# Hybrid S5, RG-LRU and GLA block: another order at the first norm, the decay logarithms, the GLA heads and the turn of the feed-forward part

## The chip, the cores and the metric

One core of one Trainium2 chip runs the kernel. The metric is the device time of one execution in microseconds (us), lower is better. Five engines work side by side and wait for each other by semaphores: TensorE (PE, the matmuls), VectorE (DVE), ScalarE (ACT), GpSimd (POOL) and SyncE (SP, which here only issues DMAs). Each takes its instructions in one order fixed beforehand, so an instruction that waits holds up all that stand behind it on its engine.

## What is computed

One layer over 1024 latent tokens and 256 context tokens of width 1024, in float32:

```python
u  = modulate(rms_norm(h, ln1_g), mod[0], mod[1])        # mod = split(silu(c) @ ada_w + ada_b)
zl = split(u @ w_in);  zc = split(uc @ w_in)             # 5408 columns
s5_l  = s5_branch(zc[0], zl[0], ...)                     # 16 groups x 64 complex states, both directions
lru_l = rglru_branch(zc[1], zc[2], zl[1], zl[2], ...)
gla_l = gla_branch(q, k, v, g, z, ...)                   # 4 heads, chunks of 64, both directions
#   log_alpha(z) = log_sigmoid(z @ w2 + b2) / 16
#   per chunk: cum = cumsum(log_alpha); k_out = k * exp(cum_last - cum);  s = decay * s + k_out^T v
m = sigmoid(g0) * (s5_l @ w_s5) + sigmoid(g1) * (lru_l @ w_lru) + sigmoid(g2) * (gla_l @ w_gla)
h = h + mod[2] * (m @ w_out)
u = modulate(rms_norm(h, ln2_g), mod[3], mod[4])
gate, val = split(dwconv(u @ w_up))                      # 2 x 2816 channels
h = h + mod[5] * ((silu(gate) * val) @ w_down)
return rms_norm(h, final_g)
```

## The kernel before

Every float32 operand of a matmul is held as two parts, a rounded high part (`uh`, `wh`) and the remainder (`ul`, `wl`), and a product is three matmuls (high by high, high by low, low by high). The high part of a weight block is a copy with rounding on ACT (L214), the low part a subtraction on POOL or DVE (L215). Tokens lie in two halves of 512 columns, the width in eight tiles of 128 rows.

The program goes through these stages. Times are those of the profiled execution.

- **Start (0 to 41 us).** `START` is a list of steps that fixes the order on all engines by hand. `x` loads a tile, `sq` squares it on ACT, `sa` adds the squares (L389; on DVE, for three steps of the second half on POOL, list `ONPOOL`). `rs`, `re`, `rp`, `rb`, `rc` make the inverse root and spread it over the rows. `a` loads a block of the modulation weights, `ar` multiplies one row of them (eight blocks, L310), `at`, `ac`, `am` turn it into shift and scale. `un` scales a tile (L314), `u` rounds it (L317), `ul` takes the remainder (L320), `m1` and `m2` are the first products (L428, L429).
- **Projections with three mixers.** The projections come from a generator, `proj_stream`, a list of steps each with a cost in us. Whoever builds a mixer calls `F(name)` with a number from the table `FILL`, and `fill` runs so many us of that stream at this place; this lays projection matmuls among the mixer's matmuls on PE. A weight block is taken from a queue of three (`take`).
- **z, v and the decay logarithms (194 to 336 us).** `z_steps` loads the weight block `wz`, splits it (L687, L688), multiplies context (L691, L692) and latent tokens (L699 to L701), and leaves z in SBUF. `v_steps` multiplies v for a list of blocks of 128 tokens: for each half of v it takes two weight blocks at once and fills two PSUM tiles `p` at a time (L726 to L728), then copies them out (L733) and writes them with a DMA on ACT's queue (L734). `decay_logs` runs 12 sets: one matmul `w2` by z (L653), absolute value, relu and exponential on ACT (L658, L660, L661), a polynomial as pairs of a square on ACT (L665) and a multiply-add on DVE (L662, L666), a subtraction on POOL (L667) and a write (L668). `background` strings the sets together, the 512-wide ones first; `advance` runs one step of it after each `BG` us of the stream.
- **S5 (from 335 us).** Transposes (L1166), products and outputs (L1187, L1215, L1245) with long chains on DVE, ACT and back. Logs and S5 share DVE.
- **GLA heads (519 to 900 us).** For each head `decays` runs two scans of 64x1280 (L1287, L1288), copies, exponentials (L1295 to L1297) and `ko` = exp (L1299, L1300). `states` runs 18 dependent steps on DVE (L1362) and copies the states (L1365, L1366). `nxt.decays()` of the next head is called after `head.scores(0)`. Projections go on beside it: L528 to L532 the products, L795 their evacuation by ACT through a tanh.
- **Output projection and second norm (900 to 930 us).** L284 to L286 multiply, L1722 adds to `h`. At `m == 1` of the second half the loop makes the normed first half, and POOL subtracts tiles 0 to 3 from tiles 4 to 7 (L1752).
- **The turn (930 to 986 us)** goes from this into the feed-forward part. Each pair of 128-row channel tiles is built by seven products with sums of weights and of activations (a fast scheme; `Pair`, products `p1` to `p7` with operands `B11`, `B21`, `B22`, `T1` to `T4`). The order on DVE, ACT and POOL is written by hand there (`norm_order`). `c1`, `z6`, `z57` copy and add PSUM results into `gv`; in `z57` the first instruction is a copy on ACT (L1666).
- **Main loop and end (986 to 1600 us)**: pairs 2 to 21, the down product, the last norm.

## Time and profile before

| | us |
|---|---|
| median of 3 runs | 1599.78 |
| lowest, highest | 1599.44, 1605.92 |
| the profiled execution | 1601.49 |
| its span, first to last instruction | 1599.7 |
| PE busy | 1521.8 (95%) |
| DVE busy | 1092.8 (68%) |
| ACT busy | 770.1 (48%) |
| POOL busy | 461.3 (29%) |
| mean granted clock of TensorE | 0.983 |

The span is what the trace shows; 1.8 us of the execution lie around it. PE is busy nearly all the time, so the time is that of PE's matmuls and of the places where PE waits or runs at the lower clock. The table of waits names for each wait the instruction that waited and the one that released it. A granted clock of 1.00 is 2.4 GHz, 0.50 is 1.2 GHz.

### The profile page before, as it was taken

The page shows a single profiled execution, that of the slowest core. Times are in us where ns is not written, and L with a number is a line of the kernel's source. Part 1 is how long each engine was busy: PE and PEld are TensorE (multiplying, and loading weights), DVE is VectorE, ACT ScalarE, POOL GpSimd, SP SyncE. Part 2 cuts the span into 40 slices and gives each one's busy share as a digit, 9 for nine tenths or more (in the row PEclk, how much of TensorE's full clock was granted, in tenths as well). Part 3 has the DMA queues.
Part 4 walks back from the last instruction along what each step waited for, and adds up shares of the span by engine and source line. Part 5 has one row for each costly group of instructions (what it writes and reads, how often), then busy time and mean ns, then how long its engine had stood idle before and what let it go on. Part 6 is the DMA issues. An engine that isn't in the chain of part 4 may idle for free. (4 is left out here: it accounts for less than half of the span.)

```text
span 1599.7 us, 21566 instructions
## 1 busy us (share of the span) xinstructions
PE 1521.8 (95%) x8144; PEld 1254.7 (78%) x8144; DVE 1092.8 (68%) x1620; ACT 770.1 (48%) x1221; POOL 461.3 (29%) x291
## 2 busy tenths in 40 slices
PE   5999999799998999999999988999999999999997
PEld 4888867677886788788888767788888888878887
DVE  4533469879876624533461689888888888899962
ACT  4423766665543643443233455444444444444661
POOL 3313333431122323222236534333333333000032
PEclk9999999899999999999999999999999999999999
DMA  9763633221224244231474321222222222974203
GB/s 346 242 224 93 208 109 110 93 90 58 64 61 144 70 139 130 77 86 60 144 246 159 130 88 40 92 80 79 80 91 81 80 80 100 370 248 157 93 27 106
DMA packets 93785, 198.91 MB, mean 124 GB/s; under 512 B 13489, under 2 KB 34865, under 8 KB 93553
## 3 DMA queue, kind: packets, MB, share of 16 engines
q1 hardware_dynamic: 81968, 181.62, 33.9%
q10 hardware_dynamic: 11712, 15.91, 2.9%
q8 instruction: 64, 1.05, 0.3%
q14 instruction: 41, 0.33, 0.1%
HBM read 158.98 MB, written 38.52 MB: 123 GB/s over the span
## 5 line engine op out<-in xcount | busy, mean ns | idle before, releaser
L215 POOL TENSOR_TENSOR wl<-wr,wh 128x1024 fp32r<-128x1024 f32 (+2 forms) x87 | 183.4, 2109 | 455.7 <-ACT wh L214 428.5
L214 ACT CAST wh<-wr 128x1024 fp32r<-128x1024 f32 (+2 forms) x87 | 77.3, 891 | 139.6 <-issue 41.9
L215 POOL TENSOR_TENSOR wp<-tmp,wp 128x512 fp32r<-128x512 f32 x44 | 74.1, 1701 | 220.4 <-ACT wp L214 203.4
L528 PE MATMUL ma<-uh,wh 128*128 128x512 f32 x272 | 118.0, 434 | 4.5 <-ACT pt L795 4.5
L528 PE MATMUL mb<-uh,wh 128*128 128x512 f32 x272 | 107.2, 394 | 0.0
L530 PE MATMUL ma<-ul,wh 128*128 128x512 f32 x272 | 107.0, 393 | 0.0
L530 PE MATMUL mb<-ul,wh 128*128 128x512 f32 x272 | 106.9, 393 | 0.0
L532 PE MATMUL mb<-uh,wl 128*128 128x512 f32 x272 | 106.7, 392 | 0.0
L532 PE MATMUL ma<-uh,wl 128*128 128x512 f32 x272 | 106.4, 391 | 0.0
L214 ACT CAST wp<-tmp 128x512 fp32r<-128x512 f32 x78 | 46.5, 619 | 93.0 <-DVE tmp L1629 92.9
L1693 DVE SCALAR_TENSOR_TENSOR ca<-gv,vec,ca 128x1023 f32<-128x1023 f32 (+2 forms) x66 | 61.4, 954 | 23.7 <-ACT ca L1685 23.6
L214 ACT CAST wp<-hd 128x512 fp32r<-128x512 f32 x88 | 52.8, 618 | 49.1 <-PE bkd L1998 25.9
L214 ACT CAST wp<-wr 128x512 fp32r<-128x512 f32 x97 | 58.2, 620 | 36.4 <-DMA wr<-in_wdn_dram 17.4
L1696 DVE SCALAR_TENSOR_TENSOR ca<-gv,vec,ca 128x1023 f32<-128x1023 f32 (+2 forms) x66 | 70.6, 1093 | 0.1
L528 PEld LDWEIGHTS ma<-uh,wh 128*128 128x128 f32 x272 | 51.8, 190 | 20.7 <-issue 6.5
L2178 POOL TENSOR_TENSOR acc<-acc,tmp 128x256 f32<-128x256 f32 (+1 forms) x9 | 9.0, 1002 | 182.8 <-ACT tmp L2175 182.7
L215 DVE TENSOR_TENSOR wp<-hd,wp 128x512 fp32r<-128x512 f32 x88 | 60.7, 708 | 1.3 <-ACT wp L214 1.1
L530 PEld LDWEIGHTS ma<-ul,wh 128*128 128x128 f32 x272 | 51.6, 190 | 11.5
L532 PEld LDWEIGHTS ma<-uh,wl 128*128 128x128 f32 x272 | 51.4, 189 | 11.5
L532 PEld LDWEIGHTS mb<-uh,wl 128*128 128x128 f32 x272 | 51.3, 189 | 11.4
L530 PEld LDWEIGHTS mb<-ul,wh 128*128 128x128 f32 x272 | 51.3, 189 | 11.3
L528 PEld LDWEIGHTS mb<-uh,wh 128*128 128x128 f32 x272 | 52.0, 191 | 9.5 <-issue 1.4
(628 smaller groups left out, 4661.9 us busy)
## 6 DMA issues: line engine op xcount, KB each, us to landing
wa<-in_ada_dram SPq DMA_DIRECT2D x96, 256.0 KB
wr<-in_wup_dram SPq DMA_DIRECT2D x46, 512.0 KB
wr<-in_win_dram SPq DMA_DIRECT2D x40, 512.0 KB
wr<-in_wdn_dram SPq DMA_DIRECT2D x22, 512.0 KB
hd<-hid SPq DMA_DIRECT2D x22, 512.0 KB
hid<-ca SPq DMA_DIRECT2D x21, 512.0 KB
wr<-in_wout_dram SPq DMA_DIRECT2D x16, 512.0 KB
tmp<-in_wdn_dram SPq DMA_DIRECT2D x22, 256.0 KB
```

The costliest lines, as they stand in the source:

```text
L214: S.copy(h, src)
L215: lo.tensor_tensor(l, src, f32(h), OP.subtract)
L528: PE.matmul(p[j], h[:, kk], uh[j][:, k], start=f, stop=False)
L530: PE.matmul(p[j], h[:, kk], ul[j][:, k], start=False, stop=False)
L532: PE.matmul(p[j], l[:, kk], uh[j][:, k], start=False, stop=e)
L1693: V.scalar_tensor_tensor(a[:, t0_ + 1:t0_ + 1 + n1], x[:, o:o + n1], fw[0], a[:, t0_ + 1:t0_ + 1 + n1], OP.mult, OP.add)
L1696: V.scalar_tensor_tensor(a[:, t0_ + c - 1:t0_ + n - 1], x[:, o + c:o + n], fw[2], a[:, t0_ + c - 1:t0_ + n - 1], OP.mult, OP.add)
L2178: G.tensor_tensor(acc, acc, sq, OP.add)
```

## The change

Six places are changed; the number and kind of matmuls stays the same (6571 rows on PE before and after).

1. `START`: a new order. `ONPOOL` is gone, all squares are added on DVE (one square gets a buffer of its own, `sqp`). A row of modulation weights is multiplied in two pieces, six blocks and two (`ar(r, 0, 6)`, `ar(r, 6, 8)`), the first before the spreading of the inverse root. Scaling, rounding and first product of tiles 0 and 1 of the first half stand ahead of squares 3 to 7 of the second half.
2. `z_prep` is split off `z_steps` and runs at the marker "lru"; its parts lie in a `tmp` buffer and in two halves of `lsw[2]`.
3. `decay_logs`: `BG` is 6 instead of 4, the context sets (256 wide) come first, and the relu part gets its own buffer `lsw[3]` in place of a `tmp`. `v_steps` takes one weight block at a time and holds four PSUM tiles (for the latent blocks) through both.
4. The next head's `decays` carry the order "not before the last state step" (`issue_after(head.last.ins)`).
5. The four subtractions L1752 move to DVE, to `m == 3`.
6. Turn: `q[1].p1()` before the sums, the two `B21` products apart from each other and each behind a piece of the norm, a new method `c57` holding the copy that was first in `z57`, called earlier; `q[1].p3()` before `q[0].p4()`. In the main loop `c57` stands right before `z57`, as before.

```diff
-BG = 4
+BG = 6
-ONPOOL = [('sq', 2, 1), ('sq', 4, 1), ('sq', 6, 1)]
...
-    def ada_rows(r, p):
-        for k, w in enumerate(ada.pop(r)):
+    def ada_rows(r, p, k0=0, k1=KT):
+        for k in range(k0, k1):
+            w = ada[r][k]
...
-            (G if ("sq", k, j) in ONPOOL else V).tensor_tensor(accs1[j], accs1[j], sqs[k, j], OP.add)
+            V.tensor_tensor(accs1[j], accs1[j], sqs[k, j], OP.add)
...
-            r = tmp()[:, :n]
+            r = lsw[3][:, par * 512:par * 512 + n]
...
     def background():
-        zs, w2 = zw[0]
+        zs, zc, w2 = zw[0]
+        yield from decay_logs(0, 256, zc, w2[0])
         for j in range(2):
-            yield from decay_logs(C + j * 512, 512, zs[j], w2)
-        yield from decay_logs(0, 256, zs[2], w2)
+            yield from decay_logs(C + j * 512, 512, zs[j], w2[j])
...
+    def z_prep():
         wz = wraw(I["wz"], 256)
-        zh, _ = whl()
-        zz = zh[:, 0:512].rearrange("p (k m) -> p k m", k=KT)
-        w2 = lsw[3][0:64, 256:768]
-        SY.dma_start(w2, I["w2"])
+        zz = tmp([128, 512], F32R).rearrange("p (k m) -> p k m", k=KT)
+        w2 = [lsw[2][64 * j:64 * j + 64, 512:1024] for j in range(2)]
+        for w in w2:
+            SY.dma_start(w, I["w2"])
...
     def v_steps(blocks):
         for hv in range(2):
-            ws = take(2)
-            for b0 in range(0, len(blocks), 4):
-                bs = blocks[b0:b0 + 4]
-                p = two()
...
+            p = [one("ab"[i % 2]) for i in range(len(blocks) // 2)]
+            for kh in range(2):
+                (h, l), = take()
+                for i, b in enumerate(blocks):
...
+                    if kh and i % 2:
+                        t = pt()
+                        S.copy(t, p[i // 2])
...
         yield from marker("lru")
+        z_prep()
...
             for step in range(1, 19):
-                V.scalar_tensor_tensor(Sd[:, step], Sd[:, step - 1], self.dec[:, step:step + 1], Sd[:, step],
-                                       OP.mult, OP.add)
+                self.last = V.scalar_tensor_tensor(Sd[:, step], Sd[:, step - 1], self.dec[:, step:step + 1],
+                                                   Sd[:, step], OP.mult, OP.add)
...
         if nxt:
-            nxt.decays()
+            with tc.issue_after(head.last.ins):
+                nxt.decays()
...
+        def c57(self):
+            S.copy(self.gv[1][:, tl[0]], self.C)
+
         def z57(self):
             w, z = self.gv[1][:, tl[0]], self.gv[1][:, tl[1]]
-            S.copy(w, self.C)
...
             if j == 1 and m == 3:
+                for k in range(4, KT):
+                    x = hT[k][:, tl[0]]
+                    V.tensor_tensor(x, x, hT[k - 4][:, tl[0]], OP.subtract)
...
-                    if k > 3:
-                        x = hT[k][:, tl[0]]
-                        G.tensor_tensor(x, x, hT[k - 4][:, tl[0]], OP.subtract)
...
+    q[1].p1()
     q[1].sums((5,))
...
-    q[1].p1()
     rq = rstd_cols(st, 4, small[:, 12:16])
+    product(q[0].A, q[0].w[2], B21, False)
...
     bcast(pr, rq, 4)
+    product(q[1].A, q[1].w[2], B21, False)
     for i in range(2):
-        product(q[i].A, q[i].w[2], B21, False)
...
     q[0].load(3, 4)
+    q[0].c57()
...
     q[1].z6()
+    q[1].c57()
     q[1].z57()
...
+    q[1].p3()
     q[0].p4()
     q[0].gate()
     q[0].out()
-    q[1].p3()
     q[1].p4()
```

On ACT, while the logs and the latent v run. `L733` is the copy of a v tile from PSUM, `L214` the rounding of a weight block that PE needs next, the others are the logs. Before:

```order
L733 COPY pt_2868<-ma_2716 128x512
L665 ACTIVATE tmp_2681<-lsw_1455,small 128x512
L660 ACTIVATE tmp_2733<-sm_2730,small 128x512
L658 ACTIVATE lsw_1455<-sm_2784,vec 128x256
L734 DMA vsp<-pt_2868 128x2x256
L665 ACTIVATE tmp_2737<-lsw_1455,small 128x512
L661 ACTIVATE lsw_1455<-lsw_1455 128x256
L733 COPY pt_2871<-mb_2717 128x512
L214 CAST wh_2876<-wr_2874 128x1024
```

The same place in the changed kernel (its lines are about 9 to 16 higher: L667 to L674 the logs, L749 the v copy, L213 the rounding):

```order
L213 CAST wh_2672<-wr_2670 128x1024
L674 ACTIVATE tmp_2653<-lsw_1455,small 128x512
L674 ACTIVATE tmp_2656<-lsw_1455,small 128x512
L674 ACTIVATE tmp_2659<-lsw_1455,small 128x512
L749 COPY pt_2700<-ma_2530 128x512
L749 COPY pt_2744<-mb_2531 128x512
L750 DMA vsp<-pt_2700 128x2x256
L667 ACTIVATE lsw_1455<-sm_2727,vec 128x512
L669 ACTIVATE lsw_1458<-sm_2727,small 128x512
L670 ACTIVATE lsw_1455<-lsw_1455 128x512
L750 DMA vsp<-pt_2744 128x2x256
```

A set's instructions now stand together, with the rounding of a weight block ahead of the set's three squares, and two copies of v follow one another.

On ACT in the GLA part, where the third head's states are made and the fourth head's decays begin. `L1295` to `L1300` are the decays, `L1418` a write of an output, `L795` the two copies through which PE's next two PSUM tiles come free. Before:

```order
L1295 ACTIVATE gl_6000<-gl_5997 64x20
L1296 ACTIVATE gl_6000<-gl_5997 64x4
L1297 ACTIVATE gl_6000<-gl_5997 64x16
L1418 DMA yosp<-gl_5662 128x1024
L1300 ACTIVATE gl_6004<-gl_6004 128x1280
L795 ACTIVATE pt_6013<-ma_5857 128x512
L795 ACTIVATE pt_6014<-mb_5858 128x512
L214 CAST wh_6019<-wr_6017 128x256
L1365 COPY gl_5877<-gl_5878 64x1024
L1366 COPY gl_5877<-gl_5878 64x1024
```

The same place in the changed kernel (L1382, L1383 copy the states, L812 is the evacuation, L1312 to L1317 the decays):

```order
L1435 DMA yosp<-gl_5649 128x1024
L812 ACTIVATE pt_6000<-ma_5844 128x512
L812 ACTIVATE pt_6001<-mb_5845 128x512
L1383 COPY gl_5864<-gl_5865 64x1024
L1382 COPY gl_5864<-gl_5865 64x1024
L213 CAST wh_6006<-wr_6004 128x256
L213 CAST wh_6030<-wr_6028 128x1024
L1312 ACTIVATE gl_5987<-gl_5984 64x20
L1313 ACTIVATE gl_5987<-gl_5984 64x4
L1314 ACTIVATE gl_5987<-gl_5984 64x16
L1424 DMA acc_6221<-gsp 128x512
L1317 ACTIVATE gl_5991<-gl_5991 128x1280
```

The evacuation no longer stands behind the exponential of 128x1280; two state copies (L1382, L1383, the rows just ahead of these) stand ahead of it now, and the decays come behind the other two.

On ACT at the turn, where the operands `B22` and `T4` are rounded (L1812) and pair 0's product sum `bkc` is copied (L1666). Before:

```order
L1812 CAST B22h<-h_7296 128x512
L214 CAST wp_8205<-wr_8110 128x512
L214 CAST wp_8208<-tmp_8203 128x512
L214 CAST wp_8225<-pt_7881 128x512
L214 CAST wp_8228<-acc_8106 128x512
L1812 CAST B22h<-h_7298 128x512
L1812 CAST B22h<-h_7300 128x512
L1812 CAST T4h<-h_7294 128x512
L1812 CAST T4h<-h_7296 128x512
L1812 CAST T4h<-h_7298 128x512
L1812 CAST T4h<-h_7300 128x512
L1666 COPY gv_7990<-bkc_8039 128x512
```

The same place in the changed kernel (L1834 the rounding, L1684 the copy):

```order
L1834 CAST B22h<-h_7281 128x512
L1834 CAST B22h<-h_7283 128x512
L213 CAST wp_8192<-wr_8097 128x512
L213 CAST wp_8195<-tmp_8190 128x512
L213 CAST wp_8212<-pt_7868 128x512
L213 CAST wp_8215<-acc_8093 128x512
L1684 COPY gv_7990<-bkc_8038 128x512
L1834 CAST B22h<-h_7285 128x512
L1834 CAST B22h<-h_7287 128x512
```

The copy now stands behind the second of the eight roundings instead of behind the eighth (the first row of before, the first rounding of `B22`, is left out).

## Rows read from the trace of the kernel before

**Rows 1.** Waits of PE: instruction, releaser, us in total, times, longest us
```profile
PE ma L726 <- ACT wh L214: 7.6, 1, 7.6
PE ma L428 <- ACT uh L317: 4.7, 1, 4.7
PE bkc L839 <- ACT gv L1666: 4.6, 1, 4.6
PE ma L528 <- ACT pt L795: 4.5, 2, 3.8
PE ma L691 <- DVE wh L688: 3.9, 1, 3.9
PE sm L653 <- ACT tmp L660: 3.7, 2, 2.8
...
PE sm L286 <- POOL wl L215: 2.5, 1, 2.5
PE ma L727 <- POOL wl L215: 2.4, 1, 2.4
```

**Rows 2.** Stretches: length, busy us of PE, PEld, DVE, ACT, POOL, granted clock, DMA share
```profile
245.00:312.00 67.00, 53.20 (x322) 44.60 (x321) 61.74 (x148) 44.00 (x72) 26.82 (x14) 0.90 0.32 105
312.00:351.00 39.00, 39.00 (x236) 34.03 (x235) 27.01 (x47) 28.91 (x50) 14.95 (x9) 1.00 0.28 95
351.00:400.00 49.00, 44.14 (x220) 36.52 (x220) 45.10 (x93) 25.12 (x44) 7.58 (x5) 0.93 0.22 67
```

**Rows 3.** Two stretches at the lower clock, columns as in rows 2
```profile
299.40:309.60 10.20, 4.07 (x17) 3.77 (x18) 9.04 (x18) 5.68 (x10) 5.42 (x2) 0.50 0.37 129
664.60:668.00 3.40, 3.09 (x7) 2.42 (x8) 3.24 (x8) 2.29 (x5) 0.73 (x1) 0.50 0.15 26
```

**Rows 4.** Timeline, two matmuls at the full clock: start us, us, engine, line
```profile
658.24 0.40 PE L802 MATMUL ma<-yb,wh 128*128 128x512 f32 x1
658.47 0.39 PE L802 MATMUL mb<-yb,wh 128*128 128x512 f32 x1
```

**Rows 5.** Timeline of the start, columns as in rows 4
```profile
21.15 1.27 POOL L389 TENSOR_TENSOR t<-t,t 128x512 f32<-128x512 f32 x1 [1.96 <-DVE mods L359]
21.31 2.31 DVE L314 SCALAR_TENSOR_TENSOR x<-x,mods,t 128x512 f32<-128x512 f32 x2
24.80 1.32 ACT L317 ACTIVATE uh<-x,mods 128x512 fp32r<-128x512 f32 x2
```

**Rows 6.** Timeline at z, ACT and PE
```profile
208.20 1.28 ACT L970 ACT_TABLE_LOAD   x1
209.49 1.27 ACT L970 ACTIVATE lw<-lw 128x1280 f32<-128x1280 f32 x1
212.45 0.58 ACT L733 COPY pt<-ma 128x512 f32<-128x512 f32 x1
213.23 0.63 PE L699 MATMUL ma<-uh,wh 128*64 128x512 f32 x1
```

**Rows 7.** Timeline of the logs, DVE, then ACT
```profile
250.26 2.47 DVE L662 SCALAR_TENSOR_TENSOR lsw<-lsw 128x512 f32<-128x512 f32 x1 [1.60 <-ACT lsw L661]
...
254.33 0.69 DVE L662 SCALAR_TENSOR_TENSOR lsw<-lsw 128x512 f32<-128x512 f32 x1
...
301.99 1.04 ACT L214 CAST wh<-wr 128x1024 fp32r<-128x1024 f32 x1
```

**Rows 8.** Line L668, the write of a log set: who waited for it
```profile
  ACT tmp L665: 7.2, 5
```

**Rows 9.** Timeline of the GLA part, ACT
```profile
662.97 1.27 ACT L1300 ACTIVATE gl<-gl 128x1280 f32<-128x1280 f32 x1 [4.79 <-DVE gl L1299]
```

**Rows 10.** Timeline of the output projection, POOL
```profile
905.85 1.29 POOL L1752 TENSOR_TENSOR h<-h,h 128x512 f32<-128x512 f32 x1 [0.63 <-DVE B21l L215]
907.10 5.12 POOL L215 TENSOR_TENSOR wl<-wr,wh 128x1024 fp32r<-128x1024 f32 x2
```

**Rows 11.** Timeline of the turn, ACT
```profile
974.02 0.58 ACT L1666 COPY gv<-bkc 128x512 f32<-128x512 f32 x1
```

52 lines of the change are left out of this document (29 added, 23 removed).

## The prediction

> **What bounds the kernel now.** First the split by engine (the table above): PE is busy for 95% of the span, and the change leaves its matmuls as they are. So the kernel can gain only where PE stands still or runs at half clock, and I read the table of PE's waits next [rows 1]: the eight that lie at places of the change come to 34 us, each with the engine that ended it. The reader is to see that five of the eight end with ACT. Then I looked at each of these places in the timeline for what stood ahead of the releaser on its own engine, and last at the granted clock. After a long wait it falls to 0.50, the 1.2 GHz level, and stays there for a while [rows 3]. At full clock two matmuls of 512 columns start 0.23 us apart [rows 4]. In the 3.40 us stretch behind the wait of the GLA part 7 started, which would have taken 1.6, and 0.3 was still the wait. The low clock cost about 1.5 there. That is my price where one wait of this kind goes.
>
> **The change part by part.** Gains are positive.
>
> *Start.* PE's first product waits 4.7 us for `uh` [rows 1]. The first two scalings take 2.31 on DVE, 1.16 each, while POOL adds squares, and `uh` starts at 24.80 behind squares on ACT [rows 5]. A multiply-add of that shape takes 0.69 on DVE undisturbed [rows 7]. Scaling from 21.31 at 0.69 ends at 22.0, and with no square ahead `uh` would start there, 2.8 earlier. The squares that were ahead come later, beside products. Bounds: 0, if the halves' data are what is late, and 4. I take **+2.8**.
>
> *z.* The wait of 3.9 goes [rows 1], since the parts of `wz` are ready long before. What is late next is ACT: the latent products (L699) began at 213.23, 0.2 after a v copy had freed their tile, at 212.45 for 0.58 [rows 6]. In the new order two roundings of 1.04 [rows 7] stand ahead of that copy, a rounding of a quarter the size does not, and one table load (1.28) comes later: about +0.4 for the copy. PE then finishes the narrow context products early, waits about 5 us instead of 3.9, and comes out at the low clock on the wide products, where before it was on the narrow ones. I take **-1.7**, that is 0.4 and most of 1.5, between -4 (the roundings wait for their loads) and +2.
>
> *Logs and v.* PE waits 7.6 and 2.4 for a weight block whose rounding stood on ACT behind squares that wait for DVE, and 3.7 for PSUM tiles of the logs [rows 1]. The new `v_steps` takes a block for 96 matmuls of 256 columns, at about half of 0.23 each some 11 us, and has the next one rounded by then; the sets come every 6 us of stream, not 4. That removes 13.7, and half of the 4.07 us that PE was busy in the 10.20 at low clock [rows 3], 2.0, and one more stretch at 1.5: **+17.2**.
>
> *What S5 gives back.* S5 needs the end of DVE's log work. From 245 to 400 us DVE was busy 61.7, 27.0 and 45.1, in sum 133.9 of 155 [rows 2]. Were PE to arrive 17.2 earlier, DVE would have to be busy 97% of the time. The fullest of these stretches have 92%, with chains that go to ACT and back, as S5's do. At 92% the work takes 145.5, 9.5 less than 155. So I take **-8** for the return, between -2 (the waiting of DVE in the logs was itself the wait for PE and ACT) and -17.2.
>
> Two more table loads stand on ACT in this part (32 in the order, 30 before). A load takes 1.28, and the next instruction starts at 209.49, 0.01 behind its end [rows 6]: 2.6 us of ACT in sum, which is busy 44 of 67 us there [rows 2], so I count nothing. The Trainium skill, "ScalarE: Activation LUTs", section "What ACT_TABLE_LOAD costs", gives 1283 ns for the load and 1380 ns for a drain, 2.66 us for a switch. By that page the two would be an estimated 5.3 us, and if they lay on S5's chain the return would be larger by as much. The trace agrees on the load and shows no drain behind it.
>
> *GLA heads.* PE waits 4.5 in two places for L795 on ACT, which stood behind the `ko` exponential (662.97, 1.27), itself waiting 4.79 for DVE's scans and subtraction [rows 1, 9]. In the new order scans and exponential follow the last state step, and only two state copies stand ahead of the evacuation. With 1.5 for the clock that is 6.0; I leave 0.5 for these copies: **+5.5**, between 1 and 6. The scans' result is needed only by the next head's transposes, behind this head's outputs and norms, and the projections among them hide the move; without them the exponential and what it waits for, 1.27 and 4.79, would show [rows 9].
>
> *Subtractions of h.* POOL's last of four took 1.29 until 907.1, then the remainders of two weight blocks 5.12 [rows 10], for which PE waited 2.5 [rows 1]. On DVE four of about 0.69 [rows 7] fit in its idle time. **+4.0** with the clock, between 2 and 4.
>
> *Turn.* PE waits 4.6 for the copy of 974.02 [rows 1, 11]. With the copy ahead of six roundings it can run as soon as PE has finished that sum, about when the wait began. But the `B21` products now stand ahead of the broadcast of the norm; twelve matmuls at 0.23 are 2.8, and DVE and ACT start the norm up to so much later; I take half, 1.4, and 1.0 for weights that are late next. **+2.2**, between -1 and 3.5.
>
> *Sum.* 2.8 - 1.7 + 17.2 - 8 + 5.5 + 4.0 + 2.2 = 22.0. Against the profiled execution, 1601.49 (its span and 1.8 around it), that is 1579.5. The median run lay 1.7 below the profiled one, so 1577.8, said as **1578**.
>
> **The rivals.**
>
> *All is given back in S5.* If DVE had no slack for S5's first groups, the whole of 17.2 returns, 9.2 more than counted: 1587. For it: 92% busy in 245 to 312 and in 351 to 400 [rows 2]. Against: 12 us idle in 312 to 351.
>
> *Hardly anything is given back.* With 2 instead of 8 the time is 1572. For it: part of DVE's busy time is port time, 2.47 us for an instruction that takes 0.69 elsewhere [rows 7], and it may shrink with another spacing.
>
> *The waits come back at another place.* The four PSUM tiles that a v pass holds, or `z`, or the roundings could stop PE as often as before; then only the GLA part and the subtractions stay, some 9.5, and with losses at z and the turn of 4 the time is about 1594, no change that can be told.
>
> *Slower: the logs' own buffer.* The relu part now has two halves, so set n+2 cannot start before the write of set n is out of its half. Before, ACT waited for such writes five times, 7.2 in sum, 1.4 each [rows 8]. The place is L669 of the last ten sets, ahead of v copies and roundings on ACT. If each wait came to 1.4 and set the clock back for 1.5, ten sets cost 29, and 1578 becomes 1607. It decides once a write has not landed 12 us, two sets, after the one before it began; SP issues them in order behind weight loads, which can hold them. Five waits in twelve sets with tiles of a common pool speak for no such length.
>
> **How the numbers follow.** The forecast (1574 to 1584) 0.50; all given back 0.24; hardly anything given back 0.13; waits elsewhere 0.09; slower 0.04. About 8 us, 0.5%, is what a measurement of this kernel can tell from no change, so faster means below 1592: 0.87, same 0.09, slower 0.04. The range of 8 in 10 reaches from 1563, with the good ends of start, turn and return together, to 1592.
>
> **What would show it.** In the new profile: no wait of PE for `wh` or `wl` in the latent v, and the waits at L653 gone. A wait of 4 to 6 us ahead of the latent z products. S5's first transposes some 17 to 20 us earlier, and new waits of PE for DVE in S5 of about 8 us in sum. No wait for the evacuation L795, none for the weight remainder in the output projection, and the low stretches behind them gone. The third product of pair 0 three to four us sooner after the second norm. I am wrong if S5's waits grow by more than 15, if waits for log writes appear on ACT, or if the GLA transposes begin to wait for `ko`.

## The result and the profile after

The changed kernel takes 1583.47 us (median of 4 runs, 1580.93 to 1587.84) against 1602.55 for the kernel before in the same series (4 runs, 1599.44 to 1605.92): a ratio of 0.9883, with a 95% interval of 0.9849 to 0.9918. It is faster, by about 1.2%; the time lies 5.5 us above the 1578 that was forecast and inside the range.

The profiled execution took 1583.19, its span 1581.4 (before 1599.7). The engines, from the page of the changed kernel (busy us, share of the span, instructions):

```profile
PE 1519.7 (96%) x8144; PEld 1250.4 (79%) x8144; DVE 1082.6 (68%) x1627; ACT 777.3 (49%) x1223; POOL 445.9 (28%) x284
```

Waits of PE in the changed kernel, columns as in [rows 1]. The line numbers are higher than before, by 9 early in the kernel and by 25 at its end: L537 was L528 (gate products), L714 was L699 (wide latent z), L742 was L726 (latent v), L749 was L733 (copy of a v tile), L856 to L858 were L839 to L841. PE has 8144 instructions in both profiles; the 6571 rows named with the change stand in neither.

```profile
PE mb L537 <- ACT pt L749: 5.4, 1, 5.4
PE ma L537 <- ACT pt L749: 5.0, 1, 5.0
PE ma L714 <- ACT pt L749: 4.9, 1, 4.9
...
PE bkc L856 <- ACT gv L1684: 2.8, 1, 2.8
PE bkb L857 <- DVE wp L214: 2.4, 1, 2.4
PE ma L437 <- ACT uh L317: 2.0, 1, 2.0
PE bkd L858 <- DVE T3l L1837: 1.4, 1, 1.4
```

Against [rows 1]: the waits of the latent v for weight blocks (7.6 and 2.4), of the logs for PSUM (3.7), for the evacuation L795 (4.5, now L812, 0.7) and for the weight remainder in the output projection (2.5) are gone. The wait at the start has gone from 4.7 to 2.0, that at z from 3.9 to 4.9. New are two waits of 5 us in the gate products, both ended by copies of v tiles on ACT.

Three stretches answer to [rows 2], columns as there; the fourth is the piece in which the two new waits lie:

```profile
245.00:312.00 67.00, 61.71 (x426) 53.55 (x424) 59.20 (x158) 39.45 (x67) 33.27 (x14) 0.98 0.29 93
312.00:351.00 39.00, 33.61 (x142) 25.02 (x142) 27.71 (x48) 36.44 (x58) 11.61 (x8) 0.86 0.32 106
351.00:400.00 49.00, 46.41 (x252) 38.87 (x251) 47.43 (x98) 27.60 (x49) 7.40 (x5) 1.00 0.26 78
...
309.00:323.00 14.00, 6.05 (x14) 4.45 (x15) 10.64 (x14) 13.44 (x21) 5.31 (x3) 0.51 0.36 122
```

PE now does in the first stretch what it had partly left for the second (61.7 us busy instead of 53.2), and loses time in the second (33.6 of 39). DVE's three numbers sum to 134.3, against 133.9 before: its load has not become denser over the whole, but in the third stretch it has (47.4 of 49).

How far PE is ahead of the kernel before, at matmuls that both kernels have (start times in the two profiled executions, us from the span's start):

| matmul | before | after | ahead |
|---|---|---|---|
| last product of the first projections (L428, L437) | 65.17 | 63.09 | 2.1 |
| first wide latent z product (L699, L714) | 213.23 | 210.92 | 2.3 |
| last of them | 225.44 | 225.56 | -0.1 |
| last latent v product (L726, L742) | 325.37 | 306.04 | 19.3 |
| first transposes of S5 (L1166, L1183) | 335.29 | 330.73 | 4.6 |
| last outputs of S5 (L1245, L1262) | 487.44 | 478.59 | 8.9 |
| first transposes of the GLA part (L1331, L1348) | 524.45 | 514.20 | 10.2 |
| last of them | 700.60 | 684.68 | 15.9 |
| first `B11` product, the turn (L839, L856) | 927.11 | 906.76 | 20.4 |
| first product behind the pairs of the main loop (L1996, L2021) | 1369.30 | 1350.51 | 18.8 |

So 19.3 us have been gained when the latent v is through, 14.8 of them are gone 25 us later, and about 4 come back inside S5. Some 2 us of the 19.3 are work put off: up to the last v product PE has done the matmuls of all twelve log sets in the kernel before and of ten in the changed one, and one set takes it 1.12 (L662 at 303.09). The return is the largest movement in the table, and the experiments are mostly about it.

What happened there can be followed back through four engines. PE first, its two waits in the timeline (in the brackets the idle time before, and what ended it):

```profile
311.56 0.79 PE L537 MATMUL ma<-uh,wh 128*128 128x512 f32 x1 [5.00 <-ACT pt L749]
317.75 0.80 PE L537 MATMUL mb<-uh,wh 128*128 128x512 f32 x1 [5.39 <-ACT pt L749]
```

ACT, the releaser, in the same timeline:

```profile
296.06 0.69 ACT L667 ACTIVATE lsw<-sm,vec 128x512 f32<-128x512 f32 x1
304.77 0.69 ACT L669 ACTIVATE lsw<-sm,small 128x512 f32<-128x512 f32 x1 [8.02 <-DMA lsp<-lsw]
...
308.92 1.28 ACT L1168 ACT_TABLE_LOAD   x1
310.21 0.83 ACT L1168 ACTIVATE s<-s,small 128x640 f32<-128x640 f32 x1
310.94 0.56 ACT L749 COPY pt<-ma 128x512 f32<-128x512 f32 x1
...
313.32 1.28 ACT L670 ACT_TABLE_LOAD   x1
...
317.13 0.56 ACT L749 COPY pt<-mb 128x512 f32<-128x512 f32 x1
```

The first v copy stands in ACT's order behind L669, the relu part of a log set, and L669 waited 8.02 us for the write of the set two before it, which held the same half of the buffer `lsw[3]`. That write was issued by SP at 302.19. It waited for POOL, whose timeline is:

```profile
284.11 1.47 POOL L676 TENSOR_TENSOR lsw<-lsw,lsw 128x512 f32<-128x512 f32 x1 [1.41 <-DVE lsw L675]
290.49 11.67 POOL L676 TENSOR_TENSOR lsw<-lsw,lsw 128x512 f32<-128x512 f32 x1 [4.92 <-DVE lsw L675]
302.13 2.35 POOL L214 TENSOR_TENSOR wl<-wr,wh 128x1024 fp32r<-128x1024 f32 x1
304.45 1.28 POOL L676 TENSOR_TENSOR lsw<-lsw,lsw 128x512 f32<-128x512 f32 x1
```

The same subtraction takes 1.28 or 1.47 us in one row and 11.67 in another. DVE, meanwhile, ran one instruction behind the other without a gap; its first pause begins behind the instruction of 300.53:

```profile
300.53 0.48 DVE L1166 TENSOR_SCALAR s<-s 128x640 f32<-128x640 f32 x1
306.08 0.69 DVE L671 SCALAR_TENSOR_TENSOR lsw<-lsw 128x512 f32<-128x512 f32 x1 [5.07 <-ACT lsw L670]
```

POOL ended at 302.16, 1.15 us after DVE's pause began, and DVE's pause lasted until ACT, which was waiting for POOL's result by way of the write, had made the next set. My theory after this reading was therefore: **the gain is given back through a chain from POOL (which does not get through beside an unbroken DVE) over the log write and ACT's L669 to the v copies.** The rival was the one of the prediction: **S5 gives it back because DVE has no more slack**, whatever ACT waits for.

### The profile page after: what moved, and what is told of

The parts are those of the page before. It is cut to its first block, busy times and chain, and to the rows that moved or that the text cites. A ratio compares the mean times of both kernels' runs of the same rounds, so it can differ in the third digit from the quotient of the medians.

```text
span 1581.4 us, 21579 instructions
## 1 busy us (share of the span) xinstructions
PE 1519.7 (96%) x8144; PEld 1250.4 (79%) x8144; DVE 1082.6 (68%) x1627; ACT 777.3 (49%) x1223; POOL 445.9 (28%) x284
## 5 line engine op out<-in xcount | busy, mean ns | idle before, releaser
L214 POOL TENSOR_TENSOR wl<-wr,wh 128x1024 fp32r<-128x1024 f32 (+2 forms) x87 | 184.9, 2127 | 464.7 <-ACT wh L213 438.3
L213 ACT CAST wh<-wr 128x1024 fp32r<-128x1024 f32 (+2 forms) x87 | 77.1, 891 | 141.0 <-issue 41.6
L214 POOL TENSOR_TENSOR wp<-tmp,wp 128x512 fp32r<-128x512 f32 x44 | 71.0, 1621 | 217.8 <-ACT wp L213 206.6
L537 PE MATMUL ma<-uh,wh 128*128 128x512 f32 x272 | 117.3, 431 | 5.7 <-ACT pt L749 5.0
L537 PE MATMUL mb<-uh,wh 128*128 128x512 f32 x272 | 107.1, 394 | 5.4 <-ACT pt L749 5.4
L213 ACT CAST wp<-wr 128x512 fp32r<-128x512 f32 x97 | 59.4, 621 | 56.0 <-PE bkc L858 23.2
L213 ACT CAST wp<-hd 128x512 fp32r<-128x512 f32 x88 | 52.8, 619 | 49.3 <-PE bkd L2023 26.1
L213 ACT CAST wp<-tmp 128x512 fp32r<-128x512 f32 x78 | 46.4, 619 | 61.0 <-DVE tmp L1648 60.9
L537 PEld LDWEIGHTS ma<-uh,wh 128*128 128x128 f32 x272 | 51.6, 190 | 20.7 <-issue 5.2
L1379 DVE SCALAR_TENSOR_TENSOR gl<-gl,gl 128x128 f32<-128x128 f32 x72 | 31.2, 434 | 52.7 <-ACT gl L1377 38.4
L537 PEld LDWEIGHTS mb<-uh,wh 128*128 128x128 f32 x272 | 51.6, 190 | 15.5 <-ACT pt L749 5.9
L214 DVE TENSOR_TENSOR wp<-hd,wp 128x512 fp32r<-128x512 f32 x88 | 60.8, 708 | 1.0 <-ACT wp L213 0.8
```

What stands on the lines that cost most here:

```text
L213: S.copy(h, src)
L214: lo.tensor_tensor(l, src, f32(h), OP.subtract)
L537: PE.matmul(p[j], h[:, kk], uh[j][:, k], start=f, stop=False)
L1379: self.last = V.scalar_tensor_tensor(Sd[:, step], Sd[:, step - 1], self.dec[:, step:step + 1], Sd[:, step], OP.mult, OP.add)
```

## The experiments

Most kernels below have one time only, and the four runs of the changed kernel alone spread over 7 us. So where only one time stands, the verdict rests on the places of the matmuls in the table above. Three kernels (e4, e7, e10) have the code of the changed kernel up to the turn; in them and in it the first transposes of S5 begin at 329.2 to 331.5, and its last outputs at 477.1 to 479.3. About 2 us is thus what such a place mostly moves by itself. It can be more: e6 and e8 also share their code up to the turn, and their S5 begins 6.7 us apart, for a reason that is told under e8. "Ahead" means ahead of the changed kernel, if nothing else is said.

**e1: the subtraction of the logs on DVE.**

```diff
-            G.tensor_tensor(r, r, acc, OP.subtract)
+            V.tensor_tensor(r, r, acc, OP.subtract)
```

> The changed kernel with the last subtraction of each log set (L676) on DVE instead of POOL; all else as in the changed kernel. In its profile one of these, on POOL at 290.49, is shown as 11.67 us, the write behind it goes out at 302.19, ACT waits 8.0 us for that write at L669, and PE then waits 5.0 and 5.4 for v copies, with 13.65 us at the low clock. Theory A (POOL did not get at its operands while DVE ran without a break from 284 to 301, and ACT, then PE, wait for the write): the 8.0 on ACT and the two waits of PE go, S5's first transposes come about 10 to 13 us sooner than 330.7, and 6 to 13 of it is left at the end of S5, as far as DVE lets it. Theory B (DVE is what S5 waits for anyway, as the prediction had it; the waits only hide it): the two waits go, but PE then waits as much in S5 for DVE, and the end of S5 moves by less than 3 us, or later, since DVE has 12 instructions of about 0.69 more.

Measured: 1577.31. S5 starts 8.4 us ahead, its last outputs are 10.0 ahead, the end 5.9 (3.6 were lost again in the GLU, behind S5). One of the two waits of 5 us for a v copy is left. ACT waits 0.3 for log writes instead of 10.2. Up to S5 DVE is busy for 95% of the time from 245 us on, more than the 92% that the prediction took as its limit (a part of this is DVE held up by POOL: at 285.54 an instruction of 0.68 took 2.87). The theory of the chain gains; that DVE's fill alone sets the return does not fit.

**e2: the relu part in a common `tmp` buffer, as before.**

```diff
-            r = lsw[3][:, par * 512:par * 512 + n]
+            r = tmp()[:, :n]
```

> The changed kernel with the relu part of a log set back in a tmp buffer (three of them, shared with the squares) instead of the two halves of lsw[3]; the subtraction stays on POOL. Theory A1 (it is the own buffer of two halves that turned a late write into a wait of ACT): ACT's 8.0 us at L669 goes, some of it comes back as waits of L674 for tmp buffers, PE's two waits shrink from 10.4 to under 4, and S5's first transposes come 6 to 13 us sooner. Theory A2 (a POOL instruction that cannot start is the root, the buffer does not matter): a wait of several us remains on ACT, at L669 or L674, and PE's waits stay above 7 in sum.

Measured: 1588.9. S5 starts 4.7 us later than in the changed kernel, its end is 5.7 later. ACT now waits at the squares, L674, for the same writes (us in total, times, longest):

```profile
ACT tmp L674 <- DMA lsp<-tmp: 12.3, 4, 5.9
```

So the wait for the write is not a property of the own buffer. That the own buffer is a gain fits these places, but one run, 1.1 above the slowest of the changed kernel, does not show it.

**e3: the v tiles of the second half begin in the other PSUM pair.**

```diff
-            p = [one("ab"[i % 2]) for i in range(len(blocks) // 2)]
+            p = [one("ab"[(i + hv) % 2]) for i in range(len(blocks) // 2)]
```

> The changed kernel with the PSUM tile of v's second half taken from the other of the two rings (tag b instead of a for the context blocks; for the latent ones the four tiles alternate the other way round). In the changed kernel the latent z products (L714) wait 4.94 us for the v copy at 210.30 and then run at the low clock for 6.8 us. Theory A (the wait at z moved, as predicted, from the weight block to a copy that stands on ACT behind a square root and its table load, and it is a matter of which tile is free): the wait goes, the low stretch with it, and the last z product comes 5 to 8 us sooner than at 225.56. Theory B (z products would wait for something else, their weights or ACT's other work): the wait stays above 3 us with another releaser. For the end of the kernel both leave open how much is given back in the logs.

Measured: 1578.78. The wait at z goes, with its stretch of low clock (a wait of 2.8 for another ACT instruction, L975, appears instead), and the last z product is 4.3 ahead. In the latent v this becomes 2.4. Of the two waits for v copies one is left, but of 8.1, behind an L669 that waited 9.1 for a write, itself behind a POOL subtraction of 10.71. S5 ends 7.1 ahead, the kernel 4.4. So z's wait is a matter of which PSUM tile the copy frees, and the chain is there in this order of work too.

**e4: the first half of the turn undone** (`q[1].p1()` behind the sums, the two `B21` products together again).

```diff
-    q[1].p1()
     q[1].sums((5,))
...
+    q[1].p1()
     rq = rstd_cols(st, 4, small[:, 12:16])
-    product(q[0].A, q[0].w[2], B21, False)
...
     bcast(pr, rq, 4)
-    product(q[1].A, q[1].w[2], B21, False)
     for i in range(2):
+        product(q[i].A, q[i].w[2], B21, False)
```

> The changed kernel with the first half of the change at the turn undone: q[1].p1() behind the sums again and the two B21 products behind the broadcast, one after the other; c57 and the earlier q[1].p3() stay. In the changed kernel the stretch from the first B11 product to the first T1 product of pair 2 takes 59.94 us, in the kernel before 60.26. Theory A (the first half puts the broadcast 0.9 us later, PE's wait of 1.56 comes back as 0.79, 0.30 and 1.43 in front of T1 and T3, and these and the low clock of 6.8 us behind them eat what c57 brings): the stretch gets 2 to 4 us shorter, about 57. Theory B (the first half is worth its 1.56, and c57 brings next to nothing since the weights of pair 1 are late): the stretch gets 1 to 2 us longer, about 61.5.

Measured: 1585.66; the stretch, from the first `B11` product to the first `T1` product of pair 2, is 60.56. The wait at the sums is back, with 2.0; the waits of the `T` products at the turn shrink in return. The stretch itself repeats well where the turn is the same: 59.88 to 59.94 in e1, e3, e6, e9 and the changed kernel (59.64 in e2, 60.90 in e12). The first half may thus be worth some 0.6 there, but the spread of 59.64 to 60.90 is wider than that. The longer way from the first `B11` product to the end of the main loop's pairs is 445.8 here and 443.8 in the changed kernel, but 443.5 to 445.7 in e1, e2, e3, e9 and e12 (449.3 in e6): beyond the stretch nothing can be told.

**e5: the kernel before with the GLA heads and the subtractions of h alone.**

```diff
-            nxt.decays()
+            with tc.issue_after(head.last.ins):
+                nxt.decays()
...
+                for k in range(4, KT):
+                    x = hT[k][:, tl[0]]
+                    V.tensor_tensor(x, x, hT[k - 4][:, tl[0]], OP.subtract)
...
-                    if k > 3:
-                        x = hT[k][:, tl[0]]
-                        G.tensor_tensor(x, x, hT[k - 4][:, tl[0]], OP.subtract)
```

> The kernel before with two parts of the change alone: the next head's decays held back until the last state step, and the four subtractions of h on DVE at m == 3. The trace of the changed kernel puts them at 5.7 (from 10.2 ahead at the first GLA transposes to 15.95 ahead at the last) and 4.4 (to 20.4 ahead at the last output projection). Theory A (each part stands by itself, as the prediction's sum has it): PE is 9.5 to 10.5 us ahead of the kernel before at the end of the output projection, with no wait for L795 of over 1 us and none for the weight remainder. Theory B (in the changed kernel a part of this is slack that the other parts made, such as DVE's or ACT's free time after an earlier S5): 4 to 8 us.

Measured: 1593.17. Against the kernel before, the GLA part brings 5.7 and the subtractions of h 4.1, so PE reaches the turn 10.9 ahead. Then the stretch of the turn, which is not changed here, takes 62.91 instead of the 60.26 of the kernel before. Behind the wait at the sums (2.0, before 1.6) the granted clock falls to 0.50 for the first half of the stretch of the first row, which it did not do there before; behind the wait of 4.6 for the copy it is low for 6.83 us, where it was for 3.40 in the kernel before. First e5, then the kernel before (columns as in [rows 2]):

```profile
922.83:929.66 6.83, 6.83 (x29) 5.62 (x28) 3.94 (x9) 2.40 (x4) 2.69 (x2) 0.75 0.46 154
963.79:970.62 6.83, 4.84 (x11) 3.80 (x12) 4.33 (x7) 3.66 (x7) 4.30 (x4) 0.50 0.00 0
```

```profile
929.00:940.00 11.00, 9.44 (x50) 7.75 (x49) 9.15 (x17) 5.93 (x11) 2.69 (x2) 1.00 0.57 202
975.20:978.60 3.40, 3.40 (x9) 2.62 (x8) 1.79 (x3) 1.96 (x4) 3.40 (x3) 0.50 0.00 0
```

So in this run more than half of what the subtractions bring is lost again at the unchanged turn.

**e6: e1 and e3 together.**

> The changed kernel with both: the subtraction of a log set on DVE (alone: PE 10.0 us ahead of the changed kernel at the end of S5, 5.9 at the end of the kernel) and the v tiles in the other ring (alone: 4.3 ahead at z, 4.5 at the end). Theory A (two places, two gains, only the GLU and the logs give some back): 13 to 15 ahead at the end of S5, 8 to 11 at the end of the kernel. Theory B (DVE now carries all of it and bounds logs and S5): 10 ahead at the end of S5, as with the subtraction alone, and 6 at the end.

Measured: 1587.14, in one run no better than the changed kernel; S5 starts 3.8 ahead, less than with either edit alone. Neither expectation held. PE waits 11.38 us in one piece for a v copy, and POOL and SP show why. POOL's two instructions of this place (remainders of weight blocks) stand in one row of 24.28 us, the first of them 21.77; SP's queue below it:

```profile
282.25 24.28 POOL L214 TENSOR_TENSOR wl<-wr,wh 128x1024 fp32r<-128x1024 f32 x2 [4.69 <-ACT wh L213]
```

```profile
304.05 0.33 SPq L204 DMA_DIRECT2D wr<-in_win_dram  x1
304.47 0.38 SPq L677 DMA_DIRECT2D lsp<-lsw  x1
```

The log write (L677) had its data at 293.6, from DVE now. It stood on SP behind a weight load that waited for POOL to let go of its buffer. ACT's L669 waited 8.79 for it. So the subtraction had left POOL, the next instruction on POOL was held instead, and the write was late by another way.

**e7: both pairs' copies early at the turn** (`q[1].c57()` moved up behind `q[0].c57()`).

```diff
     q[0].c57()
+    q[1].c57()
...
-    q[1].c57()
```

> The changed kernel with the copy c57 of pair 1 right behind that of pair 0, ahead of six roundings and of pair 1's weights. In the changed kernel PE waits 2.82 and 0.27 at pair 1's third product, the first of them for this copy, and runs at the low clock for 3.4 us behind it. Theory A (the copy was what is late next): both waits and the low stretch go, and the stretch from the first B11 product to the first T1 product of pair 2 falls from 59.94 to 55.5 to 57. Theory B (the weights of pair 1, rounded behind the same roundings, are as late): the wait shrinks by less than 1 and is ended by a weight, stretch over 59.

Measured: 1585.79; the stretch is 61.22, not shorter (60.12 with the same edit in e8 and e11). PE's wait of 2.8 for the second pair's copy becomes a wait of 1.9 for the rounding of a weight block on ACT and of 0.9 for its remainder on POOL. The copies are early enough; the weights are not.

**e8: e1, e3 and e7 together, with another number for the GLU's background work.**

```diff
-        'glu': [22.0],
+        'glu': [27.0],
```

> The changed kernel with the subtraction of a log set on DVE, the v tiles in the other ring, both copies c57 early, and 27 us of projection work ahead of the GLU products instead of 22. With the subtraction alone PE waited 4.2 and 2.6 in the GLU and its lead shrank there from 10.0 to 6.4. Theory A (each wait is its own place; projection work laid into the GLU covers what waits there): 12 to 18 us faster than the changed kernel, 1566 to 1572. Theory B (DVE bounds from the logs to the GLU, and the projection work that is used up early is missing later): 6 to 9 us faster, 1575 to 1578.

Measured in five runs: 1575.89 (1571.57 to 1578.79), 0.9826 of the kernel before, interval 0.9804 to 0.9847. That is the fastest kernel of this study, below the changed one by 7.6 us. S5 starts 10.5 ahead, the turn 8.6. One wait of 5.0 for a v copy is left.

The 27.0 changes nothing: in the traces of e6 and e8 all engines have the same instructions in the same order up to the turn, where e7's edit begins, and PE has them to the end. So the two profiles show one order of work twice. The last v product begins at 301.75 in e6 and 301.80 in e8, S5 at 326.95 and 320.24, the turn at 905.58 and 898.19. The first lasting difference of the two traces is the instruction on POOL that lasted 21.77 in e6. In e8 it has its turn at once, and the weight load and the log write behind it on SP, in the same order as in e6, go out early:

```profile
282.63 2.40 POOL L214 TENSOR_TENSOR wl<-wr,wh 128x1024 fp32r<-128x1024 f32 x1 [4.69 <-ACT wh L213]
```

```profile
288.05 0.37 SPq L204 DMA_DIRECT2D wr<-in_win_dram  x1
296.13 0.32 SPq L677 DMA_DIRECT2D lsp<-lsw  x1
```

This is the plainest sight of the chain: with nothing else changed, one held instruction on POOL put S5 off by 6.7 us, and the lead was still missing at the turn. It also means that e6's 1587.14 is not what this order of work takes each time; the five times of e8, which differs from it by e7's edit alone, all lie below 1579.

**e9: e6, with the log writes issued by ACT.**

```diff
-            SY.dma_start(lsp[h][:, o:o + n], r)
+            S.dma_start(lsp[h][:, o:o + n], r)
```

> e6 (subtraction of the logs on DVE, v tiles in the other PSUM pair) plus: the write of each log set is issued by ACT instead of SP. In e6 POOL's remainder of a weight block lasted 21.77 us (282.25 to 303.98) while DVE ran with hardly a gap until 301.8; SP's next weight load waited for it (304.05), the log write stood behind that load (304.47, its data ready at 293.6), ACT waited 8.8 us for the half it frees, and the v copies behind ACT came late (PE's wait of 11.38). Theory A (what e6 lost, it lost through the order of SP's queue): ACT's wait for the write falls below 2 us, PE's wait for v copies below 6, the end of S5 is 3 to 6 us earlier than in e6, and the time is 1579 to 1583. Theory B (POOL's held remainder stops PE anyway, by the weight block that it belongs to, or ACT now waits for DVE's subtraction at the head of the write): ACT's or PE's wait comes back under another name, 1585 to 1590.

Measured: 1580.72. POOL's remainder is held as in e6, for 20.21 us, but no L669 waits for a write, and the wait of 11.38 is gone. S5 starts 6.2 us earlier than in e6 and 10.0 ahead of the changed kernel. So what e6 lost there it lost through the write that stood behind the load on SP. But of these 6.2 only 1.5 are left at the end of S5. The two longest groups among PE's waits from 245 us to the end of the GLU:

```profile
PE mb L742 <- ACT pt L749: 4.0, 2, 2.6
PE mb L537 <- DVE pt L609: 3.6, 1, 3.6
```

The first row, two waits, is v copies again, now behind ACT's wait for DVE's subtraction; the second is a wait for DVE itself, beside S5. From its first transposes to its last outputs S5 takes 151.7 here and 151.2 in e11, but 146.3 to 147.9 in e1, e6, e8 and the changed kernel. So it is not the lead that costs here: e8 starts S5 as early and keeps what it has. The loss came with the writes on ACT.

**e10: the second half of the turn undone** (the copy back in `z57`, pair 1's third products behind pair 0's fourth).

```diff
-    q[0].c57()
...
+    q[0].c57()
     q[0].z57()
...
-    q[1].p3()
     q[0].p4()
...
     q[0].out()
+    q[1].p3()
```

> After with the second half of the turn undone: the copy of pair 0's sum stands with z57 again (behind the eight roundings), and pair 1's third products behind pair 0's fourth ones. The first half (the B21 products apart, p1 early) stays. Stretch from the first B11 product to the first T1 product of pair 2: before 60.26, after 59.94, with the first half alone undone 60.56. Theory A (the early copy is worth its wait of 4.6 and what is late next takes nearly all back): 60.5 to 61.5, with a wait of about 4 us for ACT's copy again. Theory B (the second half as it stands is itself a loss, since it brings the waits of T1 and T3 and the low clock): 57 to 59.

Measured: 1580.96; the stretch is 61.07, and PE waits for the copy as it did before:

```profile
PE bkc L856 <- ACT gv L1684: 4.1, 1, 4.1
```

So the early copy is worth about 1.1 in its stretch, hardly more than the spread there. From the first `B11` product to the end of the main loop's pairs this kernel takes 443.0, the changed one 443.8: none of the 1.1 is seen at that point.

**e11: e8, with the log writes issued by ACT** (the edit of e9).

> e8 (subtraction of the logs on DVE, v tiles in the other PSUM pair, both copies early at the turn, the GLU's background due at 27.0 instead of 22.0) plus the log writes issued by ACT instead of SP. In e8 ACT waited only 3.2 us for such writes. Theory A (what waits there are left is the price of the writes behind SP's loads): the 4.99 us wait for a v copy shrinks by 2 to 3, the median is 2 to 4 us below that of e8, 1572 to 1574. Theory B (what is left in e8 is DVE itself, which runs without a gap; writes do not matter): within 1.5 us of e8, 1574.5 to 1577.5. Theory C (the writes hold ACT up, as they wait for DVE's subtraction at ACT's head): slower than e8 by 2 to 6, 1578 to 1582.

Measured in four runs: 1579.06 (1578.88 to 1580.36), 0.9852 of the kernel before, interval 0.9835 to 0.9868; 3.2 above e8. The writes that wait for DVE's subtraction hold ACT, and the last v product is 7.7 us later than in e8. PE waits 3.1 for the same DVE line as in e9.

**e12: the changed kernel, with DVE made to stop for POOL in each set.**

```diff
             G.tensor_tensor(r, r, acc, OP.subtract)
+            V.tensor_scalar(r[:, 0:1], r[:, 0:1], 1.0, None, OP.mult)
```

> After with one instruction more in each log set: DVE multiplies the first column (128x1) of POOL's difference by one, so that DVE has to stop for POOL two to four instructions after the set's last multiply-add. Nothing is taken from POOL. In the runs so far POOL's long instructions of this part (11.67, 10.71, 21.77, 20.21, 9.90, 9.82 us) end 1.1 to 2.3 us after the first moment at which DVE stood still, if only for 0.03 us. Theory A (POOL does not get through while DVE runs without a gap): no subtraction L676 lasts over 3 us, since DVE stands still for it; ACT's waits for log writes fall from 10.2 to under 3 us; DVE loses 1 to 2 us a set where it has no slack; PE's two waits of 5 for v copies shrink by 3 to 6 in sum, the first transposes of S5 come 3 to 8 us sooner than in after, and the median is 1576 to 1581. Theory B (the subtraction is slow for another reason, a DMA or ACT's accesses): one subtraction still lasts 8 to 12, now with DVE waiting for it as well, and the median is 1583 to 1592.

Measured in four runs: 1587.89 (1583.61 to 1589.52), 0.9895 of the kernel before, interval 0.9879 to 0.9912. POOL's row at the place of the 11.67:

```profile
290.14 2.08 POOL L676 TENSOR_TENSOR lsw<-lsw,lsw 128x512 f32<-128x512 f32 x1 [3.97 <-DVE lsw L675]
```

DVE stood still from 291.06, and POOL ended 1.15 later. No subtraction is held any more, and no L669 waits for a write. So the first half of theory A holds. The second half does not: S5 starts at 330.34, where it started before this edit, and PE's two waits are there as they were. Waits of PE from 290 to 340 us, and of ACT from 286 to 318 (L750 is the v copy here, L1168 and L1169, L1192 and L1197 are S5's):

```profile
PE mb L537 <- ACT pt L750: 5.7, 1, 5.7
PE ma L537 <- ACT pt L750: 4.2, 1, 4.2
```

```profile
ACT s L1197 <- DVE s L1192: 7.1, 1, 7.1
ACT s L1169 <- DVE s L1168: 3.8, 1, 3.8
```

The copies stand on ACT behind instructions of S5 that wait for DVE, and DVE has lost 6.9 us in six stops for POOL. The chain over POOL was what came last in the changed kernel; here, with 6.9 us of stops, DVE's own lateness takes its place. How late DVE would have been without these stops is not shown.

Taken together: that a held POOL instruction makes the log write late, and the write ACT, is shown (e9 takes the write away from it, e12 takes the holding away, and in both ACT's waits for writes go). That PE loses by it is shown for the order of work of e6 and e8, 6.7 us at S5's start. For the changed kernel itself it is not: e1, which takes the holding of the subtraction away without making DVE stand, starts S5 8.4 us earlier, and e12, which takes it away and makes DVE pay, starts it where it was. How the return in the changed kernel divides between the chain and DVE stays open.

## Why the prediction came out as it did

The terms of the sum, against the places of the matmuls (us gained):

| term | predicted | measured |
|---|---|---|
| start | +2.8 | +2.1 |
| z | -1.7 | -2.2 |
| logs and v, less the return | +17.2 - 8 | +9.0 |
| GLU, not in the sum | 0 | +1.4 |
| GLA heads | +5.5 | +5.7 |
| subtractions of h | +4.0 | +4.4 |
| turn, the stretch of e4 | +2.2 | +0.3 |
| main loop behind it, not in the sum | 0 | -1.9 |
| sum | 22.0 | 18.8 |

*Start and z* went as described. PE's first product began 2.65 earlier, and 0.6 of that was lost again within the first projections. At z the roundings stood ahead of the copy, as the order had shown, and the wait grew to 4.9; the granted clock was 0.50 for 6.83 us from 209.98 on, and the first wide products fell into it.

*Logs and v.* 17.2 was taken for the waits removed, and 19.4 were gained by the last v product, some 2 of them by the two log sets that come later now. The blocks did last long enough, and no product of the latent v waits for its weights.

*The return.* With the term before it, it came to 9.0 instead of 9.2; that is luck, for the step behind it was wrong. The prediction had DVE busy for 92% as a limit, and new waits of PE for DVE inside S5, some 8 us; at S5's outputs they came to 3.0, against 3.2 before. In fact PE stopped ahead of S5, twice for ACT. DVE was busy for 88% in the first stretch and 71% in the second, with a pause of 5.07 in which it waited for ACT, which waited for a write, which waited for POOL, which waited for DVE's pause. A share of busy time cannot show such a ring, in which everyone waits for the next. And 92% is no limit: e1 and e8 run at 95 and 96% up to S5. What remains of the step is that S5 can wait for DVE: in e9 and e11 PE does (3.6 and 3.1), and in e12 ACT does; but e8, as far ahead as they are, shows no such wait of PE in the gate products.

*The signs.* S5's first transposes came 4.6 us sooner, not 17 to 20, and one of the three signs of being wrong came true: ACT waited for log writes at L669, for 10.2 us. That the time still fell into the forecast is owed to what came back behind S5's start (8.9 us ahead at its end) and to the terms that stand alone. *The waits come back at another place* had part of it too: the two waits of PE are for the PSUM tiles that the v pass holds.

*The rival that ended slower* had named the place, L669 and the write two sets back, and its point, a write not landed within two sets. It happened twice, not ten times, for 10.2 us in sum. What made the write late was POOL's subtraction in the changed kernel; in e6 it was a weight load ahead of it on SP, as the rival said, but a load that itself waited for POOL. The prediction had listed POOL's subtraction nowhere on the path: it took 3.1 us at most in the kernel before, and was not followed.

*Table loads.* They were counted at nothing. In the changed kernel two of them (L1168 above at 308.92, L670 at 313.32) lie between L669's release and the copy at 317.13, 1.28 each, so up to 2.6 us of the return is theirs. The instruction behind the first one starts at 310.21, 0.01 after its end, as in [rows 6].

*GLA and the subtractions* are the two terms that e5 measured alone: 5.7 and 4.1 against 5.5 and 4.0. With no change around them they came out the same.

*Turn.* In the table this is the term that was furthest off: 0.3 came of the 2.2 that were forecast. The third product of pair 0 did begin 4.0 sooner after the first `B11` product (43.59 instead of 47.54), as forecast. What was late next was more than the 1.0 that was allowed: 2.8 for the second pair's copy, 2.4 for a weight remainder, and waits of 0.8, 0.3 and 1.4 ahead of the `T` products. (The 6.83 us at 0.50 behind these cost nothing that can be seen: in e1 and e3 only half of that was low, and the third `T2` product began 28.65 or 28.66 us after the first `B11` product in all three.) The first `T1` product of pair 2 came only 0.3 sooner. e7 shows that the weights are late right behind the copies. And e5 adds what no term had: with the turn unchanged and PE 10.9 us sooner there, this stretch took 2.65 longer, with 6.83 us more at the low clock in it. That the clock is the cause, and the sooner arrival the cause of that, is argued from one run. Against e5's 62.91 the changed turn saves 3.0, which is what the term was about; against the kernel before only 0.3 of it is seen. Of the 1.9 that are lost behind the stretch, up to the end of the main loop's pairs, the single runs of the other kernels show as much by themselves (e10 382.0, the changed kernel 383.8, e3 384.6 us for that way), so their cause is open.

*From the profiled run to the median.* The median was set 1.7 below the profiled run, as it had been in three runs of the kernel before. In the changed kernel the profiled run lies 0.3 below the median, so 2.0 of the 5.5 come from there; of the rest, 3.2 are the sum (18.8 instead of 22.0) and 0.5 was lost behind the pairs of the main loop, less the 0.2 by which 1577.8 was rounded up.

## What to carry to other kernels

When a wait is taken out of a stretch in which several engines feed each other, follow for each engine what stands behind it in order: the return here came by a buffer's write, a queue's order and a copy that stood behind both, none of which an engine's share of busy time shows. An instruction on POOL that is off the path belongs on the list as soon as DVE's row has no gap, and so does every DMA that is queued behind something that waits for POOL. Terms that stand alone (a releaser that is simply ordered too late) came out within 0.7 us; terms with a chain of the next-late things behind them did not, and there the safe value is near nothing until each of these has been priced.

## What the runs showed of the hardware

A POOL instruction that was held beside an unbroken DVE stayed held until DVE paused. In each run of the table the long instruction on POOL ends 1.1 to 2.3 us after the first moment in which DVE stood still, however short it was (so do those of 5.15 to 20.17 us in e2, e4, e7, e10 and e11); that is about the time that the instruction takes by itself (1.28 for L676, 2.35 for L214 in the rows above).

| kernel | on POOL | begins | DVE first stands still, for | ends | us |
|---|---|---|---|---|---|
| changed kernel | L676 | 290.49 | 301.01, 5.07 | 302.16 | 11.67 |
| e3 | L676 | 280.61 | 290.16, 4.57 | 291.32 | 10.71 |
| e1 | L214 | 299.20 | 306.81, 0.03 | 309.02 | 9.82 |
| e6 | L214 | 282.25 | 301.81, 0.04 | 304.02 | 21.77 |
| e9 | L214 | 284.41 | 302.36, 0.04 | 304.62 | 20.21 |
| e8 | L214 | 296.67 | 304.36, 0.04 | 306.57 | 9.90 |
| e12 | L676 | 290.14 | 291.06, 1.19 | 292.21 | 2.08 |

Not every POOL instruction is held. In the changed kernel DVE shows no gap from 273 to 301 us, and yet POOL got through in 1.43 to 1.47 at 278.43, 281.26 and 284.11. DVE's instructions of 128x32 then took 1.03 to 1.28 instead of 0.17 to 0.19. First POOL, then DVE:

```profile
278.43 1.43 POOL L1117 TENSOR_TENSOR s<-s,s 128x512 f32<-128x512 f32 x1
281.26 1.44 POOL L1121 TENSOR_TENSOR s<-s,s 128x512 f32<-128x512 f32 x1 [1.40 <-DVE s L1118]
```

```profile
278.87 1.03 DVE L1128 TENSOR_SCALAR s<-s 128x32 f32<-128x32 f32 x1
279.81 0.17 DVE L1130 TENSOR_SCALAR s<-s 128x32 f32<-128x32 f32 x1
...
281.70 1.04 DVE L1061 TENSOR_SCALAR s<-s 128x32 f32<-128x32 f32 x1
```

In e8 the instruction at 282.63 got through in 2.40, which in e6, in the same order of work, was held for 21.77. What decides whether POOL has its turn is not shown.

The other side of it is seen in e6 right behind the gap of 0.04, in DVE's timeline: POOL now has its turn, and an instruction that took 0.46 takes 2.49.

```profile
300.65 0.46 DVE L1191 TENSOR_TENSOR s<-s,s 128x288 f32<-128x288 f32 x1
...
301.85 2.49 DVE L1191 TENSOR_TENSOR s<-s,s 128x288 f32<-128x288 f32 x1
```

The Trainium skill, "SBUF — State Buffer", section "Who interferes with whom", says that a DVE instruction with two inputs in SBUF and a POOL instruction that reads SBUF exclude one another, and that whichever issues first has the shared ports for the whole instruction while the other is blocked. The DVE row of 2.49 agrees with it. The held rows of POOL go beyond it: POOL waited not for one instruction of DVE but for a whole row of them, in e6 for almost 20 us, until DVE left a gap. e12 is the test of it: a stop of 1.2 us on DVE brings the 11.67 down to 2.08.

Waits as short as 0.8, 0.3 and 1.4 us, close together, were followed by a granted clock of 0.50 (the 1.2 GHz level) for 6.83 us at the turn, in the changed kernel; in e1 and e3 it was 3.41 us at the same place:

```profile
923.36:930.19 6.83, 6.23 (x15) 4.79 (x16) 6.71 (x10) 3.45 (x5) 1.63 (x1) 0.50 0.00 0
```
